# A two-layer attention trunk on one core: weight-sum order, queue of the last turned panels, gate buffers

## The chip, the cores and the metric

The kernel runs on 1 core of one Trainium2 chip. The metric is the device time in microseconds of one execution. Five engines work at once, each through its own instructions in their written order: TensorE (PE in the profile; its weight loads are PEld), VectorE (DVE), ScalarE (ACT), GpSimd (POOL) and SyncE (SP). SyncE only issues DMA transfers here; GpSimd issues some too, and those alone can add to what lies at their destination.

## The reference

The input is 256 rows (T) of 2048 floats. Layer 1: RMS norm, one projection to q, k, v (16 heads of 128) and a forget gate for each head, normed q and k, causal softmax attention with the gate's summed logarithms as bias, output projection, residual. Then a squared-ReLU MLP. Keys and values for layer 2 come from the result; layer 2 has its own queries, attention with a learned bias by distance, projection, residual, MLP.

```
def sq_relu_mlp(h, g, w1, w2):
    a = jax.nn.relu(rms_norm(h, g) @ w1)
    return (a * a) @ w2
...
    logf = jax.nn.log_sigmoid(fz.astype(jnp.float32) + a_b_f[l].astype(jnp.float32))
    o = forgetting_attention(q, k, v, logf)
    h = h + o.reshape(B, S, D) @ a_w_out[l]
    h = h + sq_relu_mlp(h, mlp_norm_g[layer], mlp_w1[layer], mlp_w2[layer])
```

w1 is 2048 x 8192, w2 is 8192 x 2048, for each of the two MLPs.

## The kernel before, in words

**Products in three passes.** Every weight tile is split into a rounded part `hi` (ScalarE, L323) and the remainder `lo` (VectorE, L324), and so is every activation. Three groups of matmuls follow each other: x_hi with w_hi (L592), x_lo with w_hi (L594), x_hi with w_lo (L596). A tile of 128 x 1024 weights is a *unit*. A plain unit, a *panel*, covers two 128-row blocks of weights for both 128-row blocks of the input: 12 matmuls, three groups of four. The names a2 to a7 are the panels of a pair's first 512 output columns, b2 to b7 those of its second; panel number u reads the activations 2u and 2u + 1.

**Seven products instead of eight.** Weights come in *pairs* of two 512-column parts. Part of each pair is a 2 x 2 block matrix with quarters 11, 12, 21, 22, and its product is made from seven *forms* with weights 11, T3 = 22 + 12, T2 = T3 + 11, T1 = 12 + 11, 21, T4 = T2 + 21, and 22. T3 and T2 are sums of VectorE (L964, `make`). T1 and T4 are added by GpSimd's accumulating DMA (L974, `put`), which takes its second addend from DRAM. In the MLPs nearly all pairs are *deep*: the quarters are 128 x 2048, 1 MB, and a form is two units ("halves"), each of 6 matmuls, three groups of two. A deep form and a panel thus have 12 matmuls each. All sums of a pair lie in two places: T1 in that of 12, and T3, T2 and T4 in one room, which the next pair's T3 takes over.

**Order of the work.** `plan` (L180) writes the order of units by hand. Every pair begins 11, T3, T2, T1, with the panels b5, b6, b7 of the pair before between them. Then comes the pair's own line from `ORD`, in which each F is the next of the last three forms, in the order of `FO` ("456": 21, T4, 22; "465": 21, 22, T4). The MLP's chunk c has two pairs of the first product (`ahead0`, `ahead1`; the very first are `early` and `second`), which give its hidden panels n = 0 to 3, and two of the second product (`deep0`, `deep1`). They are run interleaved: second product pair 0 of chunk c, first product pair 0 of chunk c + 1, second product pair 1 of c, first product pair 1 of c + 1. Hidden panel n holds activations 4n to 4n + 3 of its chunk. The forms of a deep pair read activations 0 to 7, a4 and a5 read 8 to 11, a6 and a7 read 12 to 15, that is, n = 3.

**How far ahead.** `fetch` (in `run`, ahead of the unit's matmuls) sees to it that the conversions of the unit and of the two behind it have been issued; there are three buffers for `hi` and three for `lo`. So the conversion of the unit two on waits for the matmuls of the unit before the current one.

**Small steps between.** A list `fill` holds steps for later. One entry of it is run after each panel and after the second half of each deep form. When hidden panel n has been made, `turn_hidden` transposes it in 32 x 32 blocks on VectorE (L440) and enters its steps at the entries that the row n of table `T` gives (rows `T0H`, `T0K` for chunk 0): for n = 3, first the moves `q<-z`, 16 small DMAs half by SyncE and half by GpSimd (`hop`, L466; entry 0), and then the four steps of `take`: relu (ScalarE, L1037), square into the act tile's high part (L1042), square in place (L1044), and VectorE's subtraction that gives the low part (L1048). Entry 0 runs after T1 of the pair that follows.

**Due times.** A pair's quarters and sums are asked for by `prepare` (L976): a table for each sort of pair gives for 12, 22, 21, 11, T3 and T1 how many panels ahead of the pair's first form this is done. `QS` is that of the second query pair, `W2S` and `W2L` those of the second product's pair 1. T2 and T4 have no such time: they are made when T3 and T2 have been converted, in `issue` (L305).

**Turned panels of the residual.** `next_x` (L485) prepares the activations for the next product: after each residual panel it writes a transposed panel to DRAM (`turn<-z`, L450) and reads it back in four DMAs (`q<-turn`, L456) on SyncE's queue. For the query activations (`kept` given) the last panel, n = 3, is read by GpSimd's queue (`query<-turn`). ScalarE then scales it (L417) and splits it (L420; VectorE L421).

**Gates.** `logs` (L872) sums the four parts of the forget gates' projection from PSUM, in part through copies of ScalarE.

Of the kernel before, what the change touches and what calls it, by code (L numbers as in the profile page):

```python
# [9 lines left out]
F32 = mybir.dt.float32  # L10
F32R = mybir.dt.float32r
AF = mybir.ActivationFunctionType
# [4 lines left out]
T = 256  # L17
# [12 lines left out]
TABLES = {  # L30
    "ATA": ((10, 13, 15, 19, 9), (9, 12, 15, 18, 12), (8, 13, 15, 19, 9), (9, 9, 12, 12, 10)),
    "ATB": ((11, 12, 14, 18, 9), (9, 13, 15, 17, 11), (9, 12, 15, 17, 10), (7, 10, 12, 12, 10)),
# [14 lines left out]
    "LONG": ((0, 1, 2, 5, 9, 10, 11, 14, 14), (0, 0, 0, 4, 7, 9), (0, 0, 1, 2, 5, 5), (1, 0, 1, 4, 5, 5)),  # L47
    "OFH": (11, 10, 2, 7, 7, 6),
    "OFK": (9, 9, 4, 8, 8, 4),
# [3 lines left out]
    "OSH": (10, 7, 9, 6, 5, 1),  # L53
    "OSK": (9, 7, 4, 7, 5, 1),
    "OUTH": "F a2 a3 a4 b2 a5 b3 b4 F F G G b5 a6 a7 G b6 b7 G c2 G c3 G d2 c4 c5 c6 G c7 d3 d4",
    "OUTK": "a2 a3 F b2 a4 F b3 a5 F b4 b5 G G a6 a7 G b6 G c2 b7 G d2 c3 G c4 c5 c6 G c7 d3 d4",
    "QF": (4, 3, 2, 4, 2, 1),
    "QS": (10, 4, 4, 8, 4, 2),
    "RI": (3, 5, 7, 5),
    "SHORT": ((4, 0, 0, 4, 7, 7, 7, 8, 11), (2, 2, 3, 3, 7, 7, 8, 11, 13), (4, 0, 0, 2, 6, 6), (0, 0, 1, 2, 4, 5)),  # L60
# [13 lines left out]
    "XOH": (9, 13, 12, 11),  # L74
    "XOK": (10, 14, 12, 14),
    "XS": (0, 5, 5, 0),
# [23 lines left out]
def trunk(ctx: ExitStack, tc: tile.TileContext, xT, xr, gs, hg, bf, wgate, w_in, w_oa, w1a, w1fa, w1sa, w2fa, w2sa,  # L100
# [94 lines left out]
    def plan_mlp(w1, w1f, w1s, w2f, w2s, rest, when, more=None):  # L195
        pairs = []

        def add(w, wf, ws, i, wides, order, times, cols=WIDE):
            j = wides.index(i) if i in wides else i - sum(1 for k in wides if k < i)
            names = ("11", "12", "21", "22")  # L200
            if i in wides:
                m = 8 - cols // 512
                src = [[None] * (8 - m) + [ws[m * (2 * j + q) + u] for u in range(m)] for q in range(2)]
                big = {k: wf[4 * j + m] for m, k in enumerate(names)}
            else:
                src = [[w[16 * j + 8 * q + u] for u in range(8)] for q in range(2)]
                big = {k: src[int(k[1]) - 1][int(k[0]) - 1] for k in names}
            pairs.append(Pair(big, src, order, len(pairs) % 2 == 1, times, cols if i in wides else UN))

        rooms = {"12": "v0", "22": "k0", "11": "k1", "21": "v1"}  # L210
        seq = [(0, 0, 0), (0, 0, 1)]
        for c in range(NCH):
            seq += [(1, c, 0)] + [(0, c + 1, 0)] * (c + 1 < NCH) + [(1, c, 1)] + [(0, c + 1, 1)] * (c + 1 < NCH)
        for m, (second, c, q) in enumerate(seq):
            i = 2 * c + q
            if second:
                add(None, w2f, w2s, i, WIDE2, "deep%d" % q, TABLES["W2L" if i == 7 else "W2S" if q else "W2F"], DEEP)
            else:
                add(w1, w1f, w1s, i, WIDE1, ("second" if i == 1 else "ahead%d" % q) if i else "early", TABLES["W1E" + when] if not i else TABLES["W1I" + when] if i == 1 else TABLES["W1S" if q else "W1F"], DEEP)
            pairs[-1].at = second, c, q  # L220
        if more is not None:
            for q in range(2):
                add(more, None, None, q, (), "" if q else "query", TABLES["QS" if q else "QF"])
                pairs[-1].at = 1, NCH, q
        plan, rest = join(pairs, rooms, rest)
        return (queue(plan), rest) if more is not None else (queue(plan + rest), [])
# [78 lines left out]
    def issue(parts=1):  # L305
        form = None
        if not raws:
            load(parts)
        raw, cuts = raws.popleft()
        if not cuts:  # L310
            form, half = raw, raw.half
            assert form.name in form.pair.has, "unit early"
            if form.name in ("T3", "T2"):
                assert form.name + str(int(half)) in form.pair.has, "unit early"
            form.pair.issued.add(form.name)
            raw, cuts = form.pair.t[form.name], [slice(0, form.pair.cols - UN if half else UN)]
            if half:
                raw = raw[:, UN:]
        n = cuts[-1].stop
        hi = wsp.tile([P, n], F32R, name="hi" if n == UN else "hih", bufs=3 if n == UN else 1)  # L320
        lo = wsp.tile([P, n], F32R, name="lo" if n == UN else "loh", bufs=3 if n == UN else 1)
        for c in cuts:
            S.activation(hi[:, c], raw[:, c], AF.Copy)  # L323
            V.tensor_tensor(lo[:, c], raw[:, c], hi[:, c].bitcast(F32), op=ALU.subtract)  # L324
        ready.append((hi, lo, n < UN))
        if form and form.pair.deep and form.name == "T3":
            make(form.pair, "T2", int(half))
        elif form and form.pair.order == "second" and form.name == "T2":
            put(form.pair, "T4", int(half))
        elif form and half == form.pair.wide:  # L330
            if form.name == "T3":
                make(form.pair, "T2")
            elif form.name == "T2" and form.pair.adds:
                put(form.pair, "T4")
# [108 lines left out]
    def carry(z, dst, wait=1, reader=SY):  # L443
        w = z.shape[1]
        n = w // 4
        box = []

        def rows():
            box.append(dram.tile([P, w], F32, name="turn", tag=f"turn{w}", bufs=4))
            SY.dma_start(box[0], z)  # L450

        def columns():
            s = box[0].rearrange("(i a) f -> a i f", i=4)
            d = dst.rearrange("p (i f) -> p i f", i=4)
            for j in range(4):
                reader.dma_start(d[32 * j : 32 * j + 32], s[:, :, j * n : (j + 1) * n])  # L456

        return [[rows]] + [[]] * wait + [[columns], [], []]
# [26 lines left out]
    def next_x(n, r2, stats, which, into, kept=None, fs=None, then=None, thirds=True):  # L485
        add_h = residual(n, r2)
        zt, way = [], []
        fs = fs if n < 1 + thirds else None
        at = (LONG if kept is not None else SHORT2 if which == 4 else SHORT)[n]

        def use(flipped=False, which=which, into=into, fs=fs, tag=None):
            t = zt[1].rearrange("p (i k b c) -> p k b i c", i=4, k=GH, b=NB)
            if flipped:
                t = t[:, :, :, ::-1, ::-1]
            return split_turned(t, n, which, into, fs, tag)

        def turn():
            zt.extend((turned(), query_room(n - 1)) if kept is not None and n >= 2 else turned("q"))
            for b in range(NB):
                blocks32(h[b][:, n * 512 : (n + 1) * 512], zt[0], b)  # L500
            way.extend(i[0] for i in carry(*zt, 0, G if kept is not None and n == NG - 1 else SY)[:2])

        def rows():
            for b in range(NB):
                stats.add(b, n)

        def f(b, ps):
            add_h(b, ps)
            if b == NB - 1:
                step = steps(use)  # L510
                do = [rows, turn, lambda: way[0](), lambda: way[1](), step, step, step, step, step]
                items = [[] for _ in range(max(at) + 1)]
                for i, d in zip(at[: 6 if fs is None else 9], do):
                    items[i].append(d)
                if then is not None:
                    items[at[0] + 3].append(then)
                add_fill(items)
                if kept is not None:
                    kept.append(use)
        return f  # L520
# [328 lines left out]
    def gates(x, st):  # L849
# [22 lines left out]
        def logs():  # L872
            z = wk.tile([H, T], F32, name="gz", tag="wk")
            u = wk.tile([H, T], F32, name="gu", tag="wk")
            S.activation(z, box[0][:H, T:], AF.Copy)
            V.tensor_tensor(u, box[0][:H, :T], z, op=ALU.add)
            S.activation(z, box[0][32 : 32 + H, :T], AF.Copy)
            V.tensor_tensor(u, u, z, op=ALU.add)
            V.tensor_tensor(u, u, st.R[:H, :], op=ALU.mult)
            V.tensor_scalar(u, u, bfb, None, op0=ALU.add)  # L880
            V.scalar_tensor_tensor(z, u, -1.0, u, op0=ALU.mult, op1=ALU.max)
# [481 lines left out]
```

## Time and profile before

| | us |
|---|---|
| median of three runs (2054.76 to 2056.26) | 2055.9 |
| profiled execution, span from first to last instruction | 2051.8 |
| TensorE busy | 2042.6 |
| VectorE busy | 1784.1 |
| ScalarE busy | 1404.8 |
| GpSimd busy | 244.2 |

The profile holds one execution; its page gives the span and no other time of it. The granted TensorE clock was 1.000. A row of the timeline gives start, duration, engine, line, operation and tiles (out<-in), merged instructions as xN, and in brackets the engine's idle time before it and what ended that. A row of the waits gives who waited for whom, the total, how often, and the longest. Time in which an engine other than the bounding one is idle costs nothing by itself.

### The profile page before, as it was taken

The page shows a single profiled execution, that of the slowest core. Times are in us where ns is not written, and L with a number is a line of the kernel's source. Part 1 is how long each engine was busy: PE and PEld are TensorE (multiplying, and loading weights), DVE is VectorE, ACT ScalarE, POOL GpSimd, SP SyncE. Part 2 cuts the span into 40 slices and gives each one's busy share as a digit, 9 for nine tenths or more (in the row PEclk, how much of TensorE's full clock was granted, in tenths as well). Part 3 has the DMA queues.
Part 4 walks back from the last instruction along what each step waited for, and adds up shares of the span by engine and source line. Part 5 has one row for each costly group of instructions (what it writes and reads, how often), then busy time and mean ns, then how long its engine had stood idle before and what let it go on. Part 6 is the DMA issues. An engine that isn't in the chain of part 4 may idle for free.

```text
span 2051.8 us, 27095 instructions
## 1 busy us (share of the span) xinstructions
PE 2042.6 (100%) x9062; PEld 1688.9 (82%) x9062; DVE 1784.1 (87%) x2065; ACT 1404.8 (68%) x1805; POOL 244.2 (12%) x351
## 2 busy tenths in 40 slices
PE   9999999999999999999999999999999999999999
PEld 8888888878888888888878888888888888888887
DVE  7788798899898898899988788889988988988996
ACT  7766676677677676677778666667866676776764
POOL 1121010021111102101012111100111111111020
PEclk9999999999999999999999999999999999999999
DMA  8898888898888898898879888888988888988985
GB/s 321 259 293 273 272 279 245 306 268 266 296 258 285 259 297 271 248 292 273 264 242 300 278 256 285 258 264 286 286 290 267 271 262 289 264 287 261 295 260 149
DMA packets 175021, 557.78 MB, mean 272 GB/s; under 512 B 40592, under 2 KB 69152, under 8 KB 152096
## 3 DMA queue, kind: packets, MB, share of 16 engines
q1 hardware_dynamic: 153824, 464.99, 63.7%
q0 software_dynamic: 20768, 90.75, 22.5%
q8 instruction: 71, 1.16, 0.2%
q14 instruction: 70, 0.57, 0.1%
q10 hardware_dynamic: 288, 0.30, 0.1%
HBM read 516.07 MB, written 27.29 MB: 265 GB/s over the span
## 4 chain that ended last, share of the span: by engine, by line
PE 94%; DVE 3%; DMA 1%; ACT 1%; issue 1%; SPq 0%; ACTq 0%; POOL 0%; DVEq 0%; POOLq 0%
PE acc L596 22%; PE acc L592 22%; PE acc L594 22%; PE s L596 9%; PE s L592 9%; PE s L594 9%; DVE lo L324 1%; DMA raw<-in_w_in 1%; PE po L729 1%; PE po L766 1%; ACT hi L323 0%; PE po L767 0%; PE po L728 0%; DMA turn<-z 0%; DMA raw<-in_w_qb 0%
## 5 line engine op out<-in xcount | busy, mean ns | idle before, releaser
L324 DVE TENSOR_TENSOR lo<-raw,hi 128x1024 fp32r<-128x1024 f32 (+1 forms) x409 | 494.1, 1212 | 80.4 <-ACT hi L323 76.3
L323 ACT ACTIVATE hi<-raw 128x1024 fp32r<-128x1024 f32 (+1 forms) x409 | 429.7, 1054 | 192.2 <-PE acc L594 131.0
L592 PE MATMUL acc<-hi,act 128*128 128x512 f32 x1774 | 496.2, 392 | 1.2 <-ACT hi L323 1.1
L596 PE MATMUL acc<-lo,act 128*128 128x512 f32 x1774 | 491.1, 390 | 1.5 <-DVE lo L324 1.4
L594 PE MATMUL acc<-hi,act 128*128 128x512 f32 x1774 | 490.3, 389 | 0.0
L596 PEld LDWEIGHTS acc<-lo,act 128*128 128x128 f32 x1774 | 332.3, 188 | 73.2 <-DVE lo L324 4.2
L594 PEld LDWEIGHTS acc<-hi,act 128*128 128x128 f32 x1774 | 332.9, 188 | 69.7
L592 PEld LDWEIGHTS acc<-hi,act 128*128 128x128 f32 x1774 | 331.4, 188 | 69.8 <-ACT hi L323 1.9
L323 ACT ACTIVATE hi<-w 128x1024 fp32r<-128x1024 f32 x254 | 267.1, 1058 | 127.9 <-PE acc L594 85.2
L324 DVE TENSOR_TENSOR lo<-wT,hi 128x1024 fp32r<-128x1024 f32 x220 | 267.1, 1221 | 65.0 <-ACT hi L323 61.4
L324 DVE TENSOR_TENSOR lo<-w,hi 128x1024 fp32r<-128x1024 f32 x254 | 305.5, 1218 | 15.3 <-ACT hi L323 13.5
L323 ACT ACTIVATE hi<-wT 128x1024 fp32r<-128x1024 f32 x220 | 232.0, 1060 | 97.3 <-PE acc L594 46.2
L592 PE MATMUL s<-hi,act 128*128 128x512 f32 x530 | 146.3, 391 | 0.2 <-ACT hi L323 0.2
L596 PE MATMUL s<-lo,act 128*128 128x512 f32 x530 | 145.2, 389 | 0.4 <-DVE lo L324 0.3
L594 PE MATMUL s<-hi,act 128*128 128x512 f32 x530 | 144.8, 388 | 0.0
L466 POOL DMA_DIRECT2D q<-z x192 | 95.6, 511 | 251.8 <-DVE z L440 217.3
L596 PEld LDWEIGHTS s<-lo,act 128*128 128x128 f32 x530 | 99.0, 188 | 22.0 <-DVE lo L324 1.7
L594 PEld LDWEIGHTS s<-hi,act 128*128 128x128 f32 x530 | 99.3, 188 | 20.7
L592 PEld LDWEIGHTS s<-hi,act 128*128 128x128 f32 x530 | 98.9, 188 | 20.9 <-ACT hi L323 0.8
L596 PE MATMUL s<-lo,S 128*128 128x512 f32 x288 | 88.8, 389 | 0.7 <-DVE lo L324 0.7
L592 PE MATMUL s<-hi,S 128*128 128x512 f32 x288 | 89.4, 392 | 0.0
L594 PE MATMUL s<-hi,S 128*128 128x512 f32 x288 | 88.7, 389 | 0.0
(217 smaller groups left out, 2285.6 us busy)
## 6 DMA issues: line engine op xcount, KB each, us to landing
raw<-in_w_in SPq DMA_DIRECT2D x75, 512.0 KB, 5.8
w<-in_w2fa SPq DMA_DIRECT2D x32, 1024.0 KB, 6.5
w<-in_w2fb SPq DMA_DIRECT2D x32, 1024.0 KB, 6.0
w<-in_w1fa SPq DMA_DIRECT2D x28, 1024.0 KB, 6.9
w<-in_w1fb SPq DMA_DIRECT2D x28, 1024.0 KB, 7.6
raw<-in_w2sa SPq DMA_DIRECT2D x52, 512.0 KB, 7.4
raw<-in_w2sb SPq DMA_DIRECT2D x50, 512.0 KB, 6.8
raw<-in_w_kv SPq DMA_DIRECT2D x48, 512.0 KB, 5.1
```

Source lines behind the costliest of these rows:

```text
L323: S.activation(hi[:, c], raw[:, c], AF.Copy)
L324: V.tensor_tensor(lo[:, c], raw[:, c], hi[:, c].bitcast(F32), op=ALU.subtract)
L466: (G if i % 2 else SY).dma_start(dst[32 * j : 32 * j + 32, i * n : (i + 1) * n], z[32 * i : 32 * i + 32, j * n : (j + 1) * n])
L592: TE.matmul(ps[:, cols], xh, cut(hi, j), start=first, stop=False, **kw)
L594: TE.matmul(ps[:, cols], xl, cut(hi, j), start=False, stop=False, **kw)
L596: TE.matmul(ps[:, cols], xh, cut(lo, j), start=False, stop=last, **kw)
L729: TE.matmul(s[:, P : 3 * P], q[:, a, P:T], k[:, a], start=True, stop=True)
L766: TE.matmul(po[:, :T], v[:, 0, a * P : (a + 1) * P], pT[:, :2], start=True, stop=False)
```

## The change

Five things are changed.

- A new order `later0` stands for `deep0` from chunk 1 on: T4 comes after b4. In `ahead1` and `ahead0` T4 comes one panel later too. Row n = 3 of `T`, for chunks 1 to 3, moves the four steps of `take` by one entry.
- In `issue`, T4 of every deep pair is put in two halves, each when its half of T2 has been converted; before, only the `second` pair was done so. `W2S` and `W2L` ask for T1 two panels ahead of the pair's first form instead of one.
- The last turned panel is read by GpSimd's queue in all three places, not only for the query activations.
- `QS` asks for T3 of the second query pair three panels ahead instead of four.
- In `logs` the second copy goes to a tile of its own, `gw`, and both copies are issued ahead of the first sum.

```
-    "FO": {"second": "456", "ahead1": "456", "ahead0": "456", "deep1": "456", "deep0": "465"},
+    "FO": {"second": "456", "ahead1": "456", "ahead0": "456", "deep1": "456", "deep0": "465", "later0": "465"},
...
-    "ORD": {"second": "a4 F F a5 a6 a7 F b4", "ahead1": "a4 F F a5 a6 a7 F b4", "ahead0": "F a4 F a5 a6 a7 F b4", "deep1": "a4 F b4 F a5 F a6 a7",
+    "ORD": {"second": "a4 F F a5 a6 a7 F b4", "ahead1": "a4 F a5 F a6 a7 F b4", "ahead0": "F a4 a5 F a6 a7 F b4", "deep1": "a4 F b4 F a5 F a6 a7",
...
-        "deep0": "a4 F F F b4 a5 a6 a7"},
+        "deep0": "a4 F F F b4 a5 a6 a7",
+        "later0": "a4 F F b4 F a5 a6 a7"},
...
-    "QS": (10, 4, 4, 8, 4, 2),
+    "QS": (10, 4, 4, 8, 3, 2),
...
-    "T": ((1, -1, 5, 14, 14, 14, 15, 20, 20), (0, 2, 8, 10, 10, 14, 18, 20, 22), (0, -1, 5, 6, 7, 7), (0, -1, 4, 5, 5, 5)),
+    "T": ((1, -1, 5, 14, 14, 14, 15, 20, 20), (0, 2, 8, 10, 10, 14, 18, 20, 22), (0, -1, 5, 6, 7, 7), (0, -1, 5, 6, 6, 6)),
...
-    "W2L": (6, 5, 5, 5, 3, 1),
-    "W2S": (7, 7, 4, 5, 3, 1),
+    "W2L": (6, 5, 5, 5, 3, 2),
+    "W2S": (7, 7, 4, 5, 3, 2),
...
-                add(None, w2f, w2s, i, WIDE2, "deep%d" % q, TABLES["W2L" if i == 7 else "W2S" if q else "W2F"], DEEP)
+                add(None, w2f, w2s, i, WIDE2, "later0" if c and not q else "deep%d" % q, TABLES["W2L" if i == 7 else "W2S" if q else "W2F"], DEEP)
...
-        elif form and form.pair.order == "second" and form.name == "T2":
+        elif form and form.pair.deep and form.name == "T2":
             put(form.pair, "T4", int(half))
...
-            way.extend(i[0] for i in carry(*zt, 0, G if kept is not None and n == NG - 1 else SY)[:2])
+            way.extend(i[0] for i in carry(*zt, 0, G if n == NG - 1 else SY)[:2])
...
+            w = wk.tile([H, T], F32, name="gw", tag="wk")
             S.activation(z, box[0][:H, T:], AF.Copy)
+            S.activation(w, box[0][32 : 32 + H, :T], AF.Copy)
             V.tensor_tensor(u, box[0][:H, :T], z, op=ALU.add)
-            S.activation(z, box[0][32 : 32 + H, :T], AF.Copy)
-            V.tensor_tensor(u, u, z, op=ALU.add)
+            V.tensor_tensor(u, u, w, op=ALU.add)
```

## The prediction

> **What bounds the kernel now.** I read the page's busy times and chain first, then the waits of TensorE, then single stretches of the timeline.
>
> ```profile
> span 2051.8 us, 27095 instructions
> ...
> PE 2042.6 (100%) x9062; PEld 1688.9 (82%) x9062; DVE 1784.1 (87%) x2065; ACT 1404.8 (68%) x1805; POOL 244.2 (12%) x351
> ...
> PE 94%; DVE 3%; DMA 1%; ACT 1%; issue 1%; SPq 0%; ACTq 0%; POOL 0%; DVEq 0%; POOLq 0%
> ```
>
> TensorE is busy for 2042.6 of 2051.8 us and holds 94% of the chain. Since a busy TensorE need not be at its peak, I checked the spacing of its matmuls in one stretch, a `later0` pair to be (first MLP, chunk 1; columns are start, duration, instruction):
>
> ```profile
> 642.12 0.62 PE L592 MATMUL acc<-hi,act 128*128 128x512 f32 x2
> 643.03 0.61 PE L596 MATMUL acc<-lo,act 128*128 128x512 f32 x2
> 644.84 1.07 PE L592 MATMUL acc<-hi,act 128*128 128x512 f32 x4
> 647.56 1.07 PE L592 MATMUL acc<-hi,act 128*128 128x512 f32 x4
> 650.28 1.07 PE L592 MATMUL acc<-hi,act 128*128 128x512 f32 x4
> 651.19 1.07 PE L594 MATMUL acc<-hi,act 128*128 128x512 f32 x4
> ```
>
> Four matmuls of the panel that starts at 650.28 take until 651.19, so one every 0.227 us; panels of twelve follow each other by 2.72 us (644.84, 647.56, 650.28) with nothing between, and the form before them, two halves of six, takes 2.72 as well (642.12 to 644.84), so a half takes 1.36. The MLPs run at that pace, so a reordering there has nothing to win; it can only open a wait. What can be won is in the few waits of TensorE's weight loads:
>
> ```profile
> PEld acc L596 <- DVE lo L324: 5.7, 11, 1.8
> PEld s L596 <- DVE lo L324: 2.9, 5, 1.1
> ```
>
> These two lines hold 8.6 us in 16 waits (columns: total, times, longest), part of it while matmuls still run. 2051.8 - 2042.6 = 9.2 us is about the most that a change could take out of the span with the same matmuls. A measurement of this kernel can tell some 0.2%, 4.1 us, from no change.
>
> **The gate copies.** Before, the second copy to `gz` must wait until the sum has read the first:
>
> ```profile
> 53.87 0.36 ACT L875 ACTIVATE gz<-pg 16x256 f32<-16x256 f32 x1
> 55.07 0.37 ACT L877 ACTIVATE gz<-pg 16x256 f32<-16x256 f32 x1 [0.84 <-DVE gu L876]
> 55.35 1.04 ACT L323 ACTIVATE hi<-raw 128x1024 fp32r<-128x1024 f32 x1
> 55.34 0.61 PE L596 MATMUL s<-lo,S 128*128 128x512 f32 x2
> 56.45 1.19 PE L592 MATMUL acc<-hi,act 128*128 128x512 f32 x4 [0.49 <-ACT hi L323]
> ```
>
> The two matmuls from 55.34 end their turn at 55.34 + 2 x 0.227 = 55.79; the next starts at 56.45, right after the conversion that stands behind the gate copy on ScalarE. These 0.66 us are TensorE's loss, and 0.12 more, since the group of four then takes 1.19 instead of 1.07. With `gw` of its own the second copy follows the first, the conversion starts some 0.8 us sooner, at 54.5, ends at 55.6, and both go: -0.8 us. If the next late thing shows behind it, as little as 0; I take 0.8, since nothing else in the row waits.
>
> **The query weight sum.** `QS` lets the sum T3 of the second query pair be issued one panel later. Now VectorE stands still for it:
>
> ```profile
> 1061.77 1.22 DVE L964 TENSOR_TENSOR query<-R 128x1024 f32<-128x1024 f32 x1 [2.58 <-DMA R<-in_w_qb]
> 1062.91 1.22 DVE L324 TENSOR_TENSOR lo<-raw,hi 128x1024 fp32r<-128x1024 f32 x1
> 1070.62 1.22 DVE L324 TENSOR_TENSOR lo<-query,hi 128x1024 fp32r<-128x1024 f32 x1
> 1070.55 0.61 PE L594 MATMUL s<-hi,S 128*128 128x512 f32 x2
> 1071.89 0.74 PE L596 MATMUL s<-lo,S 128*128 128x512 f32 x2 [0.73 <-DVE lo L324]
> ```
>
> It waits 2.58 us for a weight load, then works without a gap until the `lo` of 1070.62, on which TensorE waits: due at 1070.55 + 0.45 = 1071.00, started at 1071.89, 0.89 late and 0.13 in the group (0.74 for 0.61). One panel later, the `lo` of 1062.91 runs inside the wait, and everything behind the sum moves up by one step of 1.14 us (1061.77 to 1062.91). That covers 0.89: -1.0 us, at the least -0.5.
>
> **Last turned panels on GpSimd's queue.** Each attention stage's last turned panel is read back in four DMAs. SyncE's queue spends 2.26 us on them, ScalarE waits 2.00 us for them, and the act tile is due in the panel of 402.82:
>
> ```profile
> 389.24 2.26 SPq L456 DMA_DIRECT2D q<-turn  x4
> 397.01 0.91 ACT L417 ACTIVATE y<-q,gsb 128x256 f32<-128x256 f32 x2 [2.00 <-DMA q<-turn]
> 399.70 1.06 ACT L420 ACTIVATE act<-y 128x1024 fp32r<-128x1024 f32 x1
> 402.82 1.07 PE L592 MATMUL acc<-hi,act 128*128 128x512 f32 x4
> L456 POOL DMA_DIRECT2D query<-turn x4: 550/571/602, 1047.8 to 1049.5; - x4
> query<-turn POOLq DMA_DIRECT2D x4, 128.0 KB, 4.1
> ```
>
> On GpSimd's queue four such issues take 4 x 0.57 = 2.3 us and land after 4.1; from the same 389.24 that is 395.1 against the 396.9 or so at which ScalarE is released now. `act` is read by its low part 0.9 us after 402.82, and that part ends some 1.6 us before it (399.70 + 1.06 and a subtraction of 1.2 make 402.0). The wait for the write that precedes them moves too: behind it on GpSimd's queue stands the next T1 sum, read only in the fourth form of the next pair; on SyncE's queue the weight loads move up. A later landing costs TensorE only beyond those 1.6 us, an earlier one gains nothing, as no wait of TensorE stands here: 0, at worst +0.5 twice.
>
> **Fourth sums in halves, and T1 a panel earlier.** Of 15 deep pairs in each MLP, 14 had one T4 sum of 1 MB; these 28 become two DMAs each, the first half issued one unit earlier. In `later0` and both `ahead` orders the reader stands one panel later, in `deep1` where it did. Rows that price it:
>
> ```profile
> 627.18 0.92 POOL L974 DMA_DIRECT2D wT<-in_w2fa  x1 [9.71 <-DVE lo L324]
> 634.13 3.97 POOL L466 DMA_DIRECT2D q<-z  x8 [6.03 <-DVE z L440]
> 639.15 1.06 ACT L323 ACTIVATE hi<-wT 128x1024 fp32r<-128x1024 f32 x1 [0.30 <-DMA q<-z]
> wT<-in_w2fa POOLq DMA_DIRECT2D x8, 1024.0 KB, 10.5
> R<-in_w_in POOLq DMA_DIRECT2D x5, 512.0 KB, 7.9
> ```
>
> The T4 issued at 627.18 lands 10.5 later, 637.7, 1.5 us before its conversion at 639.15. New: the second half is issued no later than the whole was, lands about 7.9 us on, 635.1, and is read one half form later, 639.15 + 1.36 = 640.5. GpSimd gets 28 x 0.92 us more to issue in 2052, in gaps of 9.71 and 6.03 like those above; the q<-z moves queue behind it for one more issue. What the halves could cost is a late T4, and that needs 5 us more here, 4 with the reader in its old place (639.15). I take 0; ends are 0, for no wait of TensorE on T4 is there to remove, and rival 3 below. T1, put on the queue one panel earlier, is behind the same T3 sum and ahead of the q<-z moves, so it lands sooner: 0. The Trainium skill, page "DMA: Bandwidth & Descriptors", section "Bandwidth", says to batch transfers to a MiB and more, and "Anatomy of one DMA" fits 2.0 us plus bytes over 436e3 to one: by it each split adds 2.0 us to its queue, and 28 would add 56 us if TensorE waited for each. The rows differ in size (10.5 for 1 MB, 7.9 for half, not 4.4 and 3.2) but agree that a half is no half price; the margin above takes it.
>
> **The new order of the deep pairs, and the hidden panels' steps.** Here the change costs. For c >= 1 the order after T1 was a4, 21, 22, T4, b4, a5, a6, a7; it becomes a4, 21, 22, b4, T4, a5, a6, a7. T's last row moves the four steps of the last hidden panel (n=3) from entries 4,5,5,5 to 5,6,6,6. An entry runs after each panel or full form, so relu went after T4 and the other three after b4; now relu goes after T4 too, which is 2.72 us later, and the other three after a5. a6 is the first panel that reads n=3. So no panel stands between the steps and their reader. The old rows:
>
> ```profile
> 643.23 1.06 ACT L323 ACTIVATE hi<-zraw 128x1024 fp32r<-128x1024 f32 x1 [0.30 <-PE acc L594]
> 644.19 1.04 ACT L1037 ACTIVATE q<-q 128x1024 f32<-128x1024 f32 x1
> 645.14 1.04 ACT L323 ACTIVATE hi<-raw 128x1024 fp32r<-128x1024 f32 x1
> 646.09 1.04 ACT L1042 ACTIVATE act<-q 128x1024 fp32r<-128x1024 f32 x1
> 647.16 1.06 ACT L1044 ACTIVATE q<-q 128x1024 f32<-128x1024 f32 x1
> 648.26 1.23 DVE L1048 TENSOR_TENSOR act<-q,act 128x1024 fp32r<-128x1024 f32 x1 [0.82 <-ACT q L1044]
> ```
>
> Old: relu 644.19, squares 646.09 and 647.16, low part 648.26 to 649.49; a6 starts at 650.28 and reads the low part with its second four matmuls at 651.19, 1.7 us to spare.
>
> New, by the same durations. A conversion runs two units ahead of its matmuls and needs the buffer of the unit before the current one: it starts 0.20 us after that unit's second group (643.23 for 643.03). T4 now fills 644.84 to 647.56. Its first half's second group ends at 644.84 + 0.91 = 645.75, so hi of a6 starts at 645.95. Behind it in ScalarE's order stand relu (+0.95 as 643.23 to 644.19) at 646.90; hi of a7, which the fetch for a5 puts there, at 647.85; square into act at 648.80; square in place (+1.07) at 649.87. VectorE's subtraction starts 1.10 later, 650.97, and ends at 652.20. TensorE is due at 651.19 and starts 0.05 later than that end (1070.62 + 1.22 = 1071.84 for 1071.89): 652.25, late by 1.06, plus about 0.11 in its group as in the two waits above: 1.17 us.
>
> It happens wherever `later0` follows a c >= 1 panel: three chunks, two MLPs, 6 x 1.17 = +7.0 us. What is queued behind: lo of a7 runs before the subtraction, the T3 sum for the next pair and its first conversions after it, and these are due only after a7, 2.72 us on, so no second wait. The ends: nothing (rival 1), and 1.17 + 1.23 = 2.4 each, +14, if one more subtraction of VectorE got ahead of it, though the written order puts none there. I take 1.17, the chain made of this stretch's own rows. The new `ahead` orders hold no hidden panel's step close to its reader: 0.
>
> **Sum.** -0.8 - 1.0 + 0 + 0 + 7.0 = +5.2. The profiled span 2051.8 becomes 2057.0. The page gives no other time of that execution; the median of the runs, 2055.9, lies 4.1 us above the span, for what is outside the first and last instruction. With the same 4.1: 2061.1.
>
> **Rivals.** (1) Not slower: the n=3 steps come in time. It needs the subtraction to end by 651.1, 1.1 us sooner than worked out: for instance if hi of a7 (0.95) ran behind the squares. Then only the two gains are left, 2055.9 - 1.8 = 2054.1. Against it: in the old rows hi of a6 and of a7 stand just where the fetch order puts them. 0.15. (2) The gains do not arrive, since the waits behind the gate copies and the query sum take their place, and the six waits do: 2055.9 + 7.0 = 2062.9. For it: 16 short waits stand close together in the rows. 0.13. (3) The halved T4, or the hops queued behind them, land late; from those 4 to 5 us of delay on it decides, and at 0.3 us in each of 28 pairs it gives 2061.1 + 8.4 = 2069.5. For it, the one 1.5 us margin above; against it, the later reader. The skill's rule on batching is of this kind. 0.06. My forecast: 0.66, its own range 2058.5 to 2063.5.
>
> **How the numbers follow.** The range leaves out rival 3 and tails of the others: 2054.0 to 2064.5. Bounds of 0.2% are 2051.8 and 2060.0. Slower by more: 0.55 of the forecast's 0.66 (six waits under 0.98 us each would fall below), all of rivals 2 and 3 less a little, 0.72. Faster: 0.03, from rival 1 with more gains than I see. The rest, 0.25.
>
> **What would show it.** Right: six waits of 1 to 1.3 us of TensorE on `act` L1048 at L594, three per MLP; hi of a7 between relu and squares on ScalarE; no wait at 55.8 and 1071; POOL sums of 512 KB, landing sooner. Wrong: no wait on L1048, or waits on conversions of wT, which would mean late T4s.

## The result and the profile after

The changed kernel takes 2067.0 us, the median of five runs, beside 2055.8 for the kernel before on the same chip: the medians are 11.1 us apart, and the ratio of the runs is 1.0056, 0.56% slower (95% interval 1.0043 to 1.0068). The direction was forecast; the time, 2061.1 with a range of 2054.0 to 2064.5, was not.

The page of after, its span and busy times:

```profile
span 2064.8 us, 27141 instructions
...
PE 2048.2 (99%) x9062; PEld 1687.2 (82%) x9062; DVE 1785.2 (86%) x2065; ACT 1405.2 (68%) x1805; POOL 277.9 (13%) x387
```

The matmuls are as many as before, and the span is 13.0 us longer. So the waits of TensorE's weight loads must tell where it went (who waits for whom, total, times, longest):

```profile
PEld acc L595 <- DVE act L1050: 8.0, 6, 1.3
PEld acc L593 <- ACT act L421: 2.8, 2, 1.9
PEld acc L593 <- issue: 2.7, 6, 0.5
```

None of the three rows has a counterpart before. The first is the forecast one; the other two, 5.5 us in eight waits, are not in the prediction. The timeline shows each at its place. First the six waits, here in chunk 1 (lines stand one or two higher than before):

```profile
648.89 1.04 ACT L1039 ACTIVATE q<-q 128x1024 f32<-128x1024 f32 x1
649.83 1.04 ACT L324 ACTIVATE hi<-raw 128x1024 fp32r<-128x1024 f32 x1
650.78 1.05 ACT L1044 ACTIVATE act<-q 128x1024 fp32r<-128x1024 f32 x1
651.86 1.06 ACT L1046 ACTIVATE q<-q 128x1024 f32<-128x1024 f32 x1
652.25 1.07 PE L593 MATMUL acc<-hi,act 128*128 128x512 f32 x4
652.95 1.23 DVE L1050 TENSOR_TENSOR act<-q,act 128x1024 fp32r<-128x1024 f32 x1 [0.82 <-ACT q L1046]
654.23 1.20 PE L595 MATMUL acc<-hi,act 128*128 128x512 f32 x4 [0.91 <-DVE act L1050]
```

The order is the one worked out: relu, `hi` of a7, the two squares, the subtraction. The second group is due at 652.25 + 0.91 = 653.16 and starts at 654.23, 1.07 late, and its group takes 0.11 to 0.13 more. Six of these make 7.1 us.

Second, the last turned panel of layer 2. The panel's first group is due at 1426.16 + 0.91 = 1427.07 and starts 0.74 later, and its next group 0.35 later than that; with what follows it is 1.2 us:

```profile
1413.23 2.28 POOL L457 DMA_DIRECT2D q<-turn  x4 [59.91 <-ACT hi L324]
1424.95 1.71 ACT L418 ACTIVATE y<-q,gsb 128x256 f32<-128x256 f32 x4 [2.96 <-DMA q<-turn]
1426.16 1.07 PE L597 MATMUL acc<-lo,act 128*128 128x512 f32 x4
1427.81 1.19 PE L593 MATMUL acc<-hi,act 128*128 128x512 f32 x4 [0.57 <-ACT act L421]
1429.07 1.20 PE L595 MATMUL acc<-hi,act 128*128 128x512 f32 x4
```

ScalarE's scaling waits 2.96 us for the reads; before, it did not wait here at all. The DMA rows of this stretch give the landing time, before on SyncE's queue:

```profile
q<-turn SPq DMA_DIRECT2D x4, 128.0 KB, 6.8
```

and after on GpSimd's:

```profile
q<-turn POOLq DMA_DIRECT2D x4, 128.0 KB, 8.8
```

The same panel of layer 1 has 1.4 us of idle time at 403.70 and 2.0 us of loss in all:

```profile
403.70 1.19 PE L593 MATMUL acc<-hi,act 128*128 128x512 f32 x4 [1.43 <-ACT act L421]
```

Third, the pairs `deep1`, where T1 is now put a panel earlier. In chunk 1, before:

```profile
692.43 3.97 POOL L466 DMA_DIRECT2D q<-z  x8 [23.46 <-DVE z L440]
698.19 0.93 POOL L974 DMA_DIRECT2D w<-in_w2fa  x1 [1.78 <-DVE lo L324]
706.95 1.05 ACT L1037 ACTIVATE q<-q 128x1024 f32<-128x1024 f32 x1
```

After:

```profile
696.68 0.50 POOL L467 DMA_DIRECT2D q<-z  x1
697.17 0.96 POOL L976 DMA_DIRECT2D w<-in_w2fa  x1
697.77 2.37 POOL L467 DMA_DIRECT2D q<-z  x4
701.93 0.50 POOL L467 DMA_DIRECT2D q<-z  x1 [1.79 <-DMA q<-z]
711.15 1.06 ACT L1039 ACTIVATE q<-q 128x1024 f32<-128x1024 f32 x1 [0.89 <-DMA q<-z]
716.30 0.70 PE L593 MATMUL acc<-hi,Sh 128*128 128x512 f32 x2
```

And the moves' DMA rows in this stretch, before and after:

```profile
q<-z SPq DMA_DIRECT2D x8, 32.0 KB, 4.5
q<-z POOLq DMA_DIRECT2D x8, 32.0 KB, 4.3
```

```profile
q<-z SPq DMA_DIRECT2D x8, 32.0 KB, 11.3
q<-z POOLq DMA_DIRECT2D x8, 32.0 KB, 9.5
```

The 1 MB sum (697.17) now stands among GpSimd's eight small moves of the hidden panel instead of behind them. The moves land 9.5 us after their issue instead of 4.3 in the median. By the trace's single landings, the three ahead of the sum are there by 702.75, the five behind it only from 708.97 on. SyncE's eight moves, which stand on another queue, are late too, 11.3 us instead of 4.5, and their last lands 0.35 us after GpSimd's last. Relu waits for them. By the order of the rows, ScalarE's conversions and a PSUM step of VectorE behind relu then come late for the matmul at 716.30; the profile itself names no releaser for that wait.

Of the gains, the query sum's came: VectorE's sum waits 1.70 us, and no matmul waits behind it, where 1.0 us was lost before:

```profile
1069.28 1.23 DVE L966 TENSOR_TENSOR query<-R 128x1024 f32<-128x1024 f32 x1 [1.70 <-DMA R<-in_w_qb]
```

The gate copies gave a third. The wait at 55.8 has gone, but a new one stands one group later:

```profile
57.09 1.07 PE L595 MATMUL acc<-hi,act 128*128 128x512 f32 x4
58.36 1.19 PE L597 MATMUL acc<-lo,act 128*128 128x512 f32 x4 [0.20 <-DVE lo L325]
```

It is due at 58.00 and comes 0.36 late, with 0.11 in its group: 0.47 in place of 0.77.

### The profile page after: what moved, and what is told of

Same layout as the page of the kernel before. It is cut to its first block, busy times and chain, and to the rows that moved or that the text cites. A ratio compares the mean times of both kernels' runs of the same rounds, so it can differ in the third digit from the quotient of the medians.

```text
span 2064.8 us, 27141 instructions
## 1 busy us (share of the span) xinstructions
PE 2048.2 (99%) x9062; PEld 1687.2 (82%) x9062; DVE 1785.2 (86%) x2065; ACT 1405.2 (68%) x1805; POOL 277.9 (13%) x387
```

## The experiments

Theory: three separate causes, namely the entries of the last hidden panel's steps, the queue of the reads, and T1's place. The rivals to each stand in the expectations.

**The steps' entries back.**

```
-"T": (..., (0, -1, 5, 6, 6, 6))
+"T": (..., (0, -1, 4, 5, 5, 5))
```

> The changed kernel, with the four steps of the last hidden panel entered as before (row n = 3 of T again 4, 5, 5, 5), so that in later0 relu runs after b4 and the other three after T4. Theory of the prediction: these steps are what the six waits of TensorE on the subtraction of L1050 come from; with a panel (a5, 2.72 us) between the steps and a6 they go, the span falls by 6 x 1.18 = 7.1 us from 2064.8 to about 2057.7, the time from 2067.0 to about 2060, and nothing late takes their place. Rival: the order later0 itself is late (T4 or the conversions around it); then four to six waits of over 0.5 us stay in these places under another name, and the span falls by less than 4 us.

Measured: ratio 1.0026 to before (1.0016 to 1.0036), median 2062.1. No wait on L1050 is left, and nothing stands in its place in the six pairs. 0.30 points are 6.2 us, near the 7.1 of the rows. The order `later0` itself leaves no wait in these places.

**The reads on SyncE's queue again.**

```
-carry(*zt, 0, G if n == NG - 1 else SY)
+carry(*zt, 0, G if kept is not None and n == NG - 1 else SY)
```

> The changed kernel, with the last turned panel of the two attention stages read by SyncE's queue again. Theory: the waits of TensorE at 401.9 and 1426.9 (2.0 and 1.2 us) come from these reads landing 8.4 us after their issue by GpSimd; they go, the reads land in about 4 us or the weight loads behind them start some 2 us later, and the span falls by 3.2 us to about 2061.6. Rival: the waits come from the weight sums put in halves or T1 asked for a panel earlier, which fill GpSimd's queue there; then the waits stay with the reads on SyncE's queue, and the span falls by less than 1 us.

Measured: 1.0039 (1.0025 to 1.0052), median 2064.4. The wait in layer 2 is gone and the reads land in 7.4 us. The one near 402 stays in part, 0.5 us and 0.45 in its groups. Neither theory as written holds for that place: it has a share that the queue does not make. The interval overlaps that of the changed kernel (1.0043 to 1.0068), so it is the rows that show this gain, not the time.

**T1 one panel ahead again.**

```
-"W2L": (6, 5, 5, 5, 3, 2), "W2S": (7, 7, 4, 5, 3, 2)
+"W2L": (6, 5, 5, 5, 3, 1), "W2S": (7, 7, 4, 5, 3, 1)
```

> The changed kernel, with T1 of the second product's pair 1 asked for one panel ahead of the pair again (last entries of W2S and W2L 1). Theory: the GpSimd half of the hops q<-z then no longer stands behind a 1 MB sum on GpSimd's queue; relu of n = 0 stops waiting about 1.9 us for it, and the waits of 0.3 to 0.45 us around 548, 551, 716, 878, 1574, 1736 and 1903 go: 2.2 us off the span, 2062.6. Rival: these waits come from the fourth sums in halves, whose second half stands on the same queue; then they stay, and the span stays within 0.7 us of 2064.8.

Measured: 1.0045 (1.0030 to 1.0061), median 2064.9. The waits of this run:

```profile
PEld acc L595 <- DVE act L1050: 8.0, 6, 1.3
PEld acc L593 <- ACT act L421: 2.7, 2, 1.7
PEld acc L593 <- issue: 0.5, 1, 0.5
```

The first two rows stay and the third falls from 2.7 to 0.5: 2.2 us, as expected. All the places named are free of waits but one, near 1734, where one wait of 1.0 us stands; before's second profile, below, has one of 1.5 us near there, behind another load, so such a wait can stand without the change, though the runs do not settle this one. Again the interval overlaps that of the changed kernel, and the rows carry the finding.

**All three back.**

> The changed kernel with all three of these taken back: the steps' entries, the reads on SyncE's queue, T1 one panel ahead. What is left of the change: the orders with a later T4, T4 in halves, the gate copies in two tiles, the query sum a panel later. Theory: the three causes are separate and add, 7.1 + 3.2 + 2.2 = 12.5 us off the span of 2064.8: 2052.3, beside 2051.8 before; by the runs about 2054.5, within 0.1% of the kernel before. Rival 1: what is left gains its 1.5 us on the waits at 55.8 and 1071, and the span is about 2050.5. Rival 2: the causes share a part (each delays the same conversions), and the span stays above 2055.

Measured: 0.9992 (0.9983 to 1.0001), median 2054.4 beside 2056.6 before on that chip. This agrees with three causes that add: taken back one by one they give 0.30, 0.17 and 0.11 points, 0.58 in sum, and together 0.64, each with an interval of some 0.1 to 0.2. The one profiled execution has a span of 2055.1, just above the 2055 at which rival 2 was to begin; 1.6 us of it is lost near 402, with the reads on SyncE's queue. What is left of the change cannot be told from nothing.

**T4 whole, T1 early.** The condition in `issue` is that of before, all else as changed.

> The changed kernel, with T4 of the deep pairs as one 1 MB sum again (only the second pair's in halves); T1 stays two panels ahead. It is the other half of the question of the run without T1's earlier place, which had no waits left at 548, 551, 716, 878 and 1903. Theory: T1's place alone makes those waits of 0.2 to 0.45 us at the pairs deep1, since its sum stands ahead of the moves q<-z on GpSimd's queue; they stay, relu at 709 still waits about 2 us, and the span stays within 1 us of 2064.8. Rival: only T1 early and halves together fill the queue that far; then the waits go, and the span falls by some 2 us to 2062.6.

Measured: 2070.5 in one run. The row `<- issue` has 2.4 us in 6 waits, nearly that of the changed kernel, so T1's place makes them without halves. The span, 2068.8, is 4 us longer than in the changed kernel, but one execution is no evidence on that, as the second profile of before will show.

**The reads on ScalarE's queue.**

```
-carry(*zt, 0, G if n == NG - 1 else SY)
+carry(*zt, 0, G if kept is not None and n == NG - 1 else S if n == NG - 1 else SY)
```

> The changed kernel, with the last turned panel of the two attention stages read by ScalarE's queue instead of GpSimd's, so that SyncE's queue is as free for its weight loads as in the changed kernel. Theory A: the reads are late since SyncE no longer waits for the write turn<-z and sends its 0.5 to 1 MB weight loads beside them; then the four reads take about 8 us here too, ScalarE's scaling waits as long, and the waits at 401.9 and 1426.9 stay at over 1 us each. Theory B: GpSimd's queue itself is slow with these reads; then they land in about 4 to 6 us from ScalarE's queue, and the wait at 1426.9 goes.

Measured: 2077.9. In both places it is worse than on GpSimd's queue; the DMA rows of layer 1 and of layer 2, and the layer-1 panel:

```profile
q<-turn ACTq DMA_DIRECT2D x4, 128.0 KB, 11.4
```

```profile
q<-turn ACTq DMA_DIRECT2D x4, 128.0 KB, 11.7
```

```profile
407.99 2.08 PE L593 MATMUL acc<-hi,act 128*128 128x512 f32 x4 [5.30 <-ACT act L421]
```

Another queue with nothing else on it is slower still, so the 4 to 6 us of theory B do not come. That speaks against GpSimd's queue as the cause without excluding it: theory A expected about 8 us, and the 3 us beyond that stay unexplained.

**One read by SyncE, three by GpSimd.**

```
-reader.dma_start(d[32 * j : 32 * j + 32], ...)
+(reader if j or reader is SY else SY).dma_start(d[32 * j : 32 * j + 32], ...)
```

> The changed kernel, with the first of the four reads of a last turned panel by SyncE's queue and the other three by GpSimd's. SyncE's queue waits for the write turn<-z again, so its weight loads start behind the write, as before the change. Theory A: with the loads held back the three reads of GpSimd land as they did from SyncE's queue, some 2 us sooner than 8.4 to 8.8, and the wait of 1.2 us at 1426.9 goes. Theory B (GpSimd's queue is slow in itself): three of the four reads are as late as in the changed kernel, and 0.8 to 1.2 us of that wait stay.

Measured: 2071.7. In layer 2 only 0.1 us of the wait is left, though GpSimd's three reads take 8.3 us, hardly less than 8.8; near 402 the whole wait stays. It does not decide: SyncE's one read costs it 0.3 to 0.5 us, and its weight loads follow at once, so the loads were hardly held back.

**SyncE held back.** This is the cleaner test of theory A.

```
             for j in range(4):
                 reader.dma_start(d[32 * j : 32 * j + 32], s[:, :, j * n : (j + 1) * n])
+            if reader is G:
...
+                for j in range(4):
+                    SY.dma_start(hold[32 * j : 32 * j + 32], box[0][32 * j : 32 * j + 32, :4])
```

> The changed kernel; behind GpSimd's four reads of a last turned panel SyncE's queue issues four reads of 128 x 4 floats in all from the same written panel into a tile that nothing reads (all three places). They move 2 KB, but SyncE waits for the write turn<-z and spends about 2 us on issuing them, as it did when it issued the reads itself; GpSimd's part is as in the changed kernel. Theory A (the freed queue's early weight loads make the reads late): the loads start some 2 us later, GpSimd's reads land in 6 to 8 us, the wait at 1426.9 (1.2 us) goes or falls under 0.4, and the one near 402 (2.0) falls to what SyncE's own reads had, 0 to 1.6. Theory B (the reads are late by GpSimd's queue): 8.4 to 8.8 us again, and 1.0 to 1.4 us at 1426.9.

Measured: 2065.4. Layer 2:

```profile
1413.01 2.52 SPq L464 DMA_DIRECT2D hold<-turn  x4
1413.72 2.28 POOL L459 DMA_DIRECT2D q<-turn  x4 [60.35 <-DMA turn<-z]
1422.30 1.71 ACT L418 ACTIVATE y<-q,gsb 128x256 f32<-128x256 f32 x4 [0.26 <-DMA q<-turn]
```

```profile
q<-turn POOLq DMA_DIRECT2D x4, 128.0 KB, 6.4
```

GpSimd's reads, still on its queue, land in 6.4 us instead of 8.8, ScalarE waits 0.26 instead of 2.96, and TensorE not at all. SyncE's next 1 MB load is issued 2.6 us after the write has landed instead of 0.6, and the last read lands 9.2 us after the write. Without the hold, six profiles with GpSimd's reads have 12.4 to 12.8 us there, and five with SyncE's reads 8.4 to 10.1, so this run is clear of the spread. In layer 2 theory A holds: what delays the reads is that SyncE, no longer waiting for the written panel, starts its weight loads beside them. Near 402 the wait stays (1.65 us idle, landing 7.9), so for that place the run does not show it.

The same landings show a smaller share that is GpSimd's own. In both layers it issues its first read 0.6 to 0.8 us after the write has landed, where SyncE takes under 0.1 us; the hold does not change that.

**The kernel before, again.**

> The kernel before, unchanged, profiled once more, to see which of its waits repeat. With the turned panel read by SyncE's queue, two experiments and the kernel with only gates and query changed had a wait of 0.1 to 1.1 us at the panel near 402 that the first profile of before has not. Theory: that wait is chance in the landing of the reads (5.8 to 8.6 us in these); here the reads land in 5.5 to 9 us and the wait is 0 to 1.2, while the waits at 55.8, 1071 (0.8 to 1.0 with their groups) and 433 (2.0) are there again to within 0.1. Rival: before never waits there, and the gate copies, the one thing that stands ahead of 402 in all of them, make it; then the reads land in under 6 us and the wait is 0.

Measured: 2057.3, span 2055.5, 3.7 us more than in the first profile. The place near 402, with SyncE's reads and nothing changed:

```profile
388.74 2.10 SPq L456 DMA_DIRECT2D q<-turn  x4
399.93 0.91 ACT L417 ACTIVATE y<-q,gsb 128x256 f32<-128x256 f32 x2 [5.73 <-DMA q<-turn]
403.73 1.20 PE L592 MATMUL acc<-hi,act 128*128 128x512 f32 x4 [1.56 <-ACT act L420]
```

```profile
q<-turn SPq DMA_DIRECT2D x4, 128.0 KB, 9.4
```

The same four reads, issued by the same queue at the same place of the program, landed in 5.8 us in one execution and in 9.4 in the other, and TensorE waited 0 or 1.56. So the wait near 402 is no work of the change alone. With the losses in the groups behind it, five profiles with SyncE's reads have 0, 0.5, 1.0, 1.6 and 2.2 us there, mean 1.1, and four with GpSimd's (after, T1 back, T4 whole, and the first variant of ScalarE's order below) 1.9 to 2.6, mean 2.2. The run with the steps' entries back (3.9) and the second variant (4.1) are left out, since the granted clock fell in these groups. The difference is 1.1 us, about the loss in layer 2, but the two groups overlap. The waits at 55.8, 1071 and 433 are there again to within 0.1. Another wait of 1.5 us ended at 1732.7 in this profile and in no other of before's kind: chance of that size can stand in a single span.

**Gates and query alone**, on the kernel before.

> The kernel before, with only the gate copies in two tiles and the query weight sum a panel later. Theory of the prediction, corrected by the changed kernel's trace: the gates give 0.3 to 0.4 us (the wait at 55.8 goes, one of 0.36 at 57.8 comes), the query sum 0.9; 2051.8 becomes about 2050.5, the time 0.06% less than before, which five rounds hardly tell from none. Rival: the later query sum only moves its wait to the conversions behind it, and the waits between 1030 and 1085 hold as much in all as the 1.6 us of the kernel before.

Measured: 0.9996 (0.9985 to 1.0007). The waits at 55.8 and 1071 are gone and nothing has taken the query's place; the gates' new wait is 0.33. Some 1.2 us by the rows is below what five rounds can tell, as the expectation says.

**ScalarE's order, two variants.** These test the prediction's chain by its arithmetic.

```
-"T": (..., (0, -1, 5, 6, 6, 6))
+"T": (..., (0, -1, 4, 6, 6, 6))     # first variant
+"T": (..., (0, -1, 5, 5, 5, 6))     # second variant
```

> The changed kernel with row n = 3 of T at 4, 6, 6, 6: relu after b4, as before, the squares and the subtraction after a5, as in the change. It tests the prediction's chain on ScalarE by its arithmetic. By it, without relu ahead the conversion of a7 starts when its buffer is free, 0.20 us after T4's second half has ended its second group (647.11 + 0.20 = 647.31 on the prediction's clock, instead of 647.85), so that the squares and the subtraction come 0.54 sooner: six waits of 1.06 - 0.54 = 0.52, and 0.11 in the group, 3.8 us in all instead of 7.1; the span about 2061.5. Rival: the entry of the last three steps alone sets it, and the six waits stay at 1.07.

Measured: 2065.2, span 2063.5, 2 us more than expected by waits elsewhere that come and go; the six waits are 0.54 us each and 0.11 in the group, against 0.52 and 0.11 worked out. The chain is right to 0.02 us.

> The changed kernel with row n = 3 of T at 5, 5, 5, 6: relu and both squares after T4, that is, ahead of the conversion of a7 in ScalarE's order; the subtraction alone after a5, as in the change. By the prediction's chain relu runs at 646.90, the squares at 647.85 and 648.80 (0.95 after the conversion's place has gone), and the subtraction from 649.9 to 651.1, just in time for the matmul due at 651.19: the six waits fall to 0 to 0.15 us, and the span to about 2058. Rival: VectorE's subtraction is late by its own entry behind a5 (another subtraction of 1.23 us stands ahead of it); then waits of 0.5 to 1.2 us stay in the six places.

Measured: 2084.8, against both. The six waits are 2.35 us, twice those of the changed kernel:

```profile
653.93 1.04 ACT L324 ACTIVATE hi<-raw 128x1024 fp32r<-128x1024 f32 x1
655.01 1.22 DVE L325 TENSOR_TENSOR lo<-raw,hi 128x1024 fp32r<-128x1024 f32 x1 [2.86 <-ACT hi L324]
656.15 1.22 DVE L1050 TENSOR_TENSOR act<-q,act 128x1024 fp32r<-128x1024 f32 x1
657.42 1.77 PE L595 MATMUL acc<-hi,act 128*128 128x512 f32 x4 [2.19 <-DVE act L1050]
```

My expectation watched ScalarE and left out VectorE's order. `lo` of a7 stands ahead of the subtraction there, and it needs `hi` of a7, which now runs behind the squares (653.93). VectorE stands still for 2.86 us, does `lo`, and only then the subtraction, one step of 1.14 us later. In size it is the upper end of the prediction (2.4 each), but by luck: that end had one more subtraction of VectorE in the way, and here the same `lo` came late. The variant also meets the condition that rival 1 gave for no loss, `hi` of a7 behind the squares; it doubled the wait.

## Why the prediction was wrong, point by point

- **What bounds the kernel, and that a reordering can only open a wait:** right.
- **The six waits, +7.0:** right in place, order and size (1.07 and 0.11 measured, 1.06 and 0.11 worked out). The run without relu ahead and the one with the entries back confirm the chain.
- **Last turned panels, 0: the first step that failed.** It said "from the same 389.24 that is 395.1 against the 396.9 or so", pricing the reads by the query panel's 4.1 us, and "on SyncE's queue the weight loads move up" as if that were free. The reads landed 7.9 to 9.5 us after issue in the profiles with GpSimd's queue as changed. In layer 2 that costs 1.2 us, and the loads that moved up are shown to be why. Near 402 it is 1.1 as a difference of means, and why is open: holding SyncE back did not help there. "The same 389.24" left out GpSimd's later start of 0.6 us as well. Together +2.3 where 0 was entered and +1.0 was the bound. The 1.6 us of room near 402 was also one execution's good fortune, as the second profile of before shows.
- **T1 a panel earlier, 0: the second.** It said "ahead of the q<-z moves, so it lands sooner: 0". That looks at T1 alone. What stood behind it, five of GpSimd's eight moves, landed behind the megabyte: +2.2 in the pairs `deep1`. That T1's place is the cause is shown, since the waits go when it is put back and stay with T4 whole. Why SyncE's moves, on a queue of their own, came late with it is not. Rival 3 had late moves, but from T4, and in all pairs.
- **T4 in halves, 0:** no loss from it shows. The changed kernel with T4 whole has the same waits in the places named, and in its one execution others besides. In the first MLP's second product a half landed 10.7 us after its issue, not the 7.9 worked out, and so no sooner than the whole before, 10.5 (row of after):

```profile
wT<-in_w2fa POOLq DMA_DIRECT2D x16, 512.0 KB, 10.7
```

  In the profile of after no wait of TensorE in that product is put down to a half, so the room for that was there.
- **Gates, -0.8:** the rows give -0.3. The next late thing showed behind it, which the lower end had allowed for.
- **Query sum, -1.0:** -0.9 to -1.0 by the rows.
- **The sum:** 7.1 + 2.3 + 2.2 - 0.3 - 0.9 = 10.4, beside 11.1 measured (8.8 to 14.0 by the interval). The remaining 0.7 is not told from chance.
- **The profiled execution:** the 4.1 us between its span and the median were not all outside the span. In every run that lists both, time and span differ by 1.7 to 1.8; the other 2.3 was, by that, a quick execution. The forecast went from the median, so its number did not suffer, but its view of the waits near 402 did.

## What to carry to other kernels

When a DMA moves to another queue, price two things besides its own landing: what the old queue will now start sooner beside it, and what on the new queue stands behind it. A megabyte put one step earlier among small moves can cost those moves much: here they landed 5 us later. Profile the kernel before twice when the sum rests on one landing time.

## What the runs showed of the hardware

A long enough wait of TensorE could cost more than itself. The variant with ScalarE's squares early has the same wait of 2.35 us six times. After the wait near 655 the granted clock fell; after the one near 823 it did not (columns: window, total, then busy time of PE, PEld, DVE, ACT, POOL, granted clock, DMA share, GB/s):

```profile
657.40:660.70 3.30, 3.28 (x9) 2.59 (x10) 2.24 (x2) 1.06 (x1) 0.94 (x1) 0.56 0.62 235
822.00:825.30 3.30, 1.16 (x6) 0.62 (x4) 2.37 (x3) 1.84 (x2) 0.00 (x0) 1.00 0.99 376
825.40:828.70 3.30, 3.30 (x15) 2.73 (x16) 3.19 (x3) 1.06 (x1) 0.93 (x1) 1.00 0.98 351
```

At a clock of 0.56 nine matmuls fit where fifteen do at 1.00, and each stood 0.20 us further from the next than the usual 0.23. This came after four of the six waits and cost up to 1.6 us each. Near 402 shorter waits did it: TensorE was 2.0 us late in this variant, 2.1 with the steps' entries back and 2.1 with the reads split, and the clock fell each time; with T4 whole it was 2.1 us late too, and the clock stayed. In the run on ScalarE's queue the clock was as low after both of its waits of about 5 us; in the first profile of before and in that of after, where TensorE was never more than 1.6 us late, it stayed at 1.00. In the traces' clock records each of these falls lasts 3.41 us, those on ScalarE's queue twice that, and the falls of one profile start whole multiples of 3.41 us apart. The Trainium skill, page "TensorE: Matmul & The Clock Gate", Part 1, puts the fall to half clock after an idle window of about 3.4 us that runs freely against the kernel. That the same wait sometimes does it and sometimes not agrees with a free-running window, and so do the multiples; that about 2 us can be enough is less than the page says, and here the measurement decides.

A second thing: the four reads landed in 5.8 to 9.4 us under one and the same order of issues, which moved a span of 2052 us by more than 1 us. Late reads went with a late load ahead of them: in the five profiles with SyncE's reads near 402, the last weight load issued before them took 6.9, 8.9, 9.5, 10.0 and 9.9 us to land, and the reads 5.8, 7.3, 8.6, 8.5 and 9.4. In the run that held SyncE back this load took 9.1 us, beside 6.5 in the profile of after, which may be why nothing was won there; that is not shown. Why the load itself is late in one execution and not in another was not tried.
